# Loading the head of x through two engines, waiting last on GpSimd, and one semaphore for TensorE's events

## The chip, the cores and the metric

The kernel runs on one core of a Trainium2 chip. The metric is the device time of one execution in microseconds. Three runs of the kernel before took 180.77, 180.64 and 180.67 us, median 180.67. Its profiled execution took 180.69 us, of which the profile shows 178.9 us, from the first instruction to the last; its mean granted TensorE clock was 0.936.

## The reference

Eight experts, each a two-layer perceptron with a ReLU between, on 256 rows of its own:

```python
n_experts, capacity, hidden, expert_hidden = 8, 256, 512, 2048
h = np.matmul(x, w1)      # [8, 256, 512] x [8, 512, 2048]
h = np.maximum(h, 0)
return np.matmul(h, w2).astype(np.float32)   # x [8, 2048, 512]
```

Inputs and output are float32. The weights are 67 MB of HBM, x and the output 4.2 MB each.

## The kernel before

All of x and all weights are brought to bf16 on their way into SBUF. GpSimd's DMA queue casts while it copies; SyncE's and ScalarE's queues copy float32 as it is.

**Loading x.** Partition p holds 16 rows of x (R = 16). The first four of them, the *head* (HEAD = 4, 128 rows of 8 KB), go through SyncE's queue as float32 into x_head, and VectorE casts them into x_sb (L116 and L117). The other twelve, the *tail*, go through GpSimd's queue and are cast on the way (L131). x_sb is not a buffer of its own: it lies in slot 2 of the buffer of w2. Only after both stands the section whose order is written by hand (L118 on); all engines enter it when the cast is done.

**Loading the weights.** GpSimd issues twelve loads, in the order of the list `loads` (L169): w1 and w2 of experts 0 and 1 together, then of 2 and 3, then smaller ones; the last, half of w2 of expert 7, has the semaphore d_half. There are four slots for each of w1 and w2 (NS = 4). A load into a used slot waits for TensorE to be done with the slot's expert (L149 to L157), and the load of w2 for experts 2 and 3 waits for the transposes, which read x_sb. SyncE waits for each landing and passes it on to TensorE as a count (L123).

**TensorE.** First 64 transposes turn x_sb into xT through PSUM (L278 on); VectorE and ScalarE each copy half of the results out (L179). Then a loop over the experts: 64 matmuls of 128x256 make the hidden layer in four groups of PSUM (h_ps, two buffers), ScalarE applies the ReLU to each group (L213) into hT, and 32 matmuls of 128x512 make the output in o_ps, which VectorE copies to out_sb (L196); the last half of expert 7 is copied by ScalarE (L219). The code of an expert is a loop whose body is issued again from registers, so all matmuls stand at L252 in the profile.

**Semaphores.** TensorE's last matmul of a transposed half raises p_xt, of a hidden group p_h, of an output half p_o. They are counters that only rise in this program, and the others wait for constants. s_ident counts the two steps of making the identity matrix, v_out two moments at which VectorE's copies are drained.

**The end.** After expert 6, GpSimd stores the outputs of seven experts in one DMA (L172, 3.6 MB); a small store of 3 KB stands ahead of it (L160). SyncE stores expert 7's output when both of its halves are copied (L125). Then GpSimd drains (L423), ScalarE waits for all stores by d_pool and d_last (L424 and L425), and the closing barrier follows, in which SyncE gathers the other engines and GpSimd clears the semaphores.

The lines that matter for the change:

```python
nc.sync.dma_start(x_head[:], x_v[:, :HEAD * H])              # L116
nc.vector.tensor_copy(x_sb[:, :HEAD * H], x_head[:])         # L117
...
pool.drain()                                                 # L423
act.wait_ge(d_pool, 48)                                      # L424
act.wait_ge(d_last, 16).then_inc(s_ident)                    # L425
```

Of the kernel before, what the change touches and what calls it, by code (L numbers as in the profile page):

```python
# [8 lines left out]
FP32 = mybir.dt.float32  # L9
BF16 = mybir.dt.bfloat16  # L10
PE = mybir.EngineType.PE


FIRST_FREE = 16512 + 8192


@with_exitstack
def kernel(
# [7 lines left out]
    nc = tc.nc  # L26
    P = 128
    E, C, H = x.shape
    F = w1.shape[2]
    MC = C // P  # L30
# [27 lines left out]
    def allot(name, shape, dtype):  # L58
# [3 lines left out]
        free += math.prod(shape[1:]) * mybir.dt.size(dtype)  # L62
        return t

    w1_sb = allot("w1_sb", [P, NS, K1 * F], BF16)
    w2_sb = allot("w2_sb", [P, NS, K2 * H], BF16)
    xT = allot("xT", [P, K1, MC, E * P], BF16)
    hT = allot("hT", [P, K2, C], BF16)
    out_sb = allot("out_sb", [P, E, MC, H], FP32)
    identity = allot("identity", [P, P], BF16)  # L70
    W1_AT, W2_AT, XT_AT = places["w1_sb"], places["w2_sb"], places["xT"]

# [7 lines left out]
    def sem(name):  # L80
        return tc.alloc_semaphore(name)

    d_w1 = [sem(f"d_w1{i}") for i in range(NS)]
    d_w2 = [sem(f"d_w2{i}") for i in range(NS)]
    d_half, d_pool, d_last = sem("d_half"), sem("d_pool"), sem("d_last")

    s_ident = sem("s_ident")
    p_xt, p_h, p_o = sem("p_xt"), sem("p_h"), sem("p_o")  # L90
    v_out, v_last = sem("v_out"), sem("v_last")

    c_xt = [sem(f"c_xt{i}") for i in range(MC)]
    c_h, c_o, c_w1, c_w2 = sem("c_h"), sem("c_o"), sem("c_w1"), sem("c_w2")
# [10 lines left out]
    loads += [(1, (E - 1,), 0, 2), (2, (E - 1,), 0, 1), (2, (E - 1,), 1, 1)]  # L105
    landed, counts = [], {}
    for w, es, h, _ in loads:
        s = d_half if h else (d_w1, d_w2)[w - 1][es[0] % NS]
        counts[id(s)] = counts.get(id(s), 0) + 16
        landed.append((s, counts[id(s)]))  # L110

# [1 line left out]

    x_pool = ctx.enter_context(tc.tile_pool(name="x_pool", bufs=1))
    x_head = x_pool.tile([P, HEAD * H], FP32, tag="x_head")
    nc.sync.dma_start(x_head[:], x_v[:, :HEAD * H])  # L116
    nc.vector.tensor_copy(x_sb[:, :HEAD * H], x_head[:])  # L117
    with tc.tile_critical(no_gpsimd_drain=True):  # L118

        sp = nc.sync  # L120
        for i, (w, es, h, n) in enumerate(loads):
# [7 lines left out]

        pool = nc.gpsimd  # L130
        pool.dma_start(x_sb[:, HEAD * H:], x_v[:, HEAD * H:]).then_inc(d_pool, 16)  # L131
        pool.memset(identity[:], 0.0).then_inc(s_ident)  # L132
        pool.wait_ge(s_ident, 1)

        pool.affine_select(  # L135
            out=identity[:],
# [3 lines left out]
            base=0,  # L140
            pattern=[[-1, P]],
            channel_multiplier=1,
        ).then_inc(s_ident)
        for i, (w, es, h, n) in enumerate(loads):


            old = es[-1] - NS
            if w == 2 and 2 in es:
                tc.wait_critical_data_deps()  # L149
                pool.wait_ge(p_xt, K1 * MC)  # L150
            if old >= 0 and h == 0:
                if w == 1:
                    pool.wait_ge(p_h, NG * (old + 1))
                else:
                    pool.wait_ge(p_o, MC * (old + 1))
            if i == len(loads) - 1:


                pool.wait_ge(v_out, 1)
                pool.dma_start(  # L160
                    out_v[:16, 0:5:2, :16], out_sb[:16, 0:5:2, 0, :16]
                ).then_inc(d_pool, 16)
            e, ne, at_slot = es[0], len(es), es[0] % NS
            if w == 2:
                src = w2_v[:, e:e + ne, h:h + n, :].rearrange("p e h n -> p e (h n)")
                dst = w2_sb[:, at_slot:at_slot + ne, h * JH * H:(h + n) * JH * H]
            else:
                src, dst = w1_v[:, e:e + ne, :], w1_sb[:, at_slot:at_slot + ne, :]
            pool.dma_start(dst, src).then_inc(landed[i][0], 16)  # L169
        pool.wait_ge(v_out, 2)  # L170
        pool.wait_ge(d_pool, 32)
        pool.dma_start(  # L172
            out_v[:, :E - 1, :], out_sb[:, :E - 1].rearrange("p e m h -> p e (m h)")
# [12 lines left out]
        dve.sem_inc(c_xt[0], 1)  # L186
        dve.sem_inc(c_o, MC)
        for ko in range(K1):
            dve.wait_ge(p_xt, ko * MC + 1)
            copy_xt(dve.tensor_copy, ko, 0).then_inc(c_xt[0])  # L190
        for e in range(E):
            for m in range(MC):
                if e == E - 1 and m == 1:
                    break
                dve.wait_ge(p_o, e * MC + m + 1)
                cp = dve.tensor_copy(out_sb[:, e, m, :], o_ps[m][:])  # L196
                cp.then_inc(v_last if e == E - 1 else c_o)
            if e in (4, E - 2):
                dve.drain().then_inc(v_out)  # L199


        act = nc.scalar
        act.sem_inc(c_xt[1], 1)
        act.sem_inc(c_h, UG - 1)
        for ko in range(K1):
            act.wait_ge(p_xt, ko * MC + 2)
            copy_xt(act.copy, ko, 1).then_inc(c_xt[1])
        for e in range(E):
            if e:
                act.wait_ge(p_o, MC * e)  # L210
            for g in range(NG):
                act.wait_ge(p_h, e * NG + g + 1)
                act.activation(  # L213
                    hT[:, g * GJ:(g + 1) * GJ, :].rearrange("p a c -> p (a c)"),
                    h_ps[g % UG][:],
                    mybir.ActivationFunctionType.Relu,
                ).then_inc(c_h)
        act.wait_ge(p_o, E * MC)
        act.copy(out_sb[:, E - 1, 1, :], o_ps[1][:]).then_inc(v_last)  # L219


# [56 lines left out]
        def transposes():  # L278
            i = 0
            for m in range(MC):  # L280
                take(c_xt[m], 1)
                for r2 in range(R // MC):
                    if i % 6 == 0:
                        for k in range(i, min(i + 6, n)):
                            row = (k % (R // MC)) * MC + k // (R // MC)
                            pe.reg_add(bank[i // 6 % 2][k - i], reg["x"], row * H * 2)
                        if i + 6 > n:
                            pe.reg_add(reg["x"], reg["x"], 2)
                    t = matmul(
                        xt_ps[m][:, r2, :],  # L290
                        at(w2_sb, bank[i // 6 % 2][i % 6], [[K1, P]]),
                        pe.lower_ap(identity[:]),
                        start_tensor_calc=True,
                        stop_tensor_calc=True,
                        is_transpose=True,
                    )
                    i += 1
                t.then_inc(p_xt)

        pe.wait_ge(s_ident, 2)  # L300
        pe.wait_ge(d_pool, 16)
        x_first = X_AT + last_column(K1)
        pe.reg_mov(reg["x"], x_first)
# [48 lines left out]
        def half():  # L352
            n = JH * K1
            for i in range(n):
                j, ko = divmod(i, K1)
                c, r = place(CHUNKS1, i)
                if i == CHUNKS1[c][1] - 2:
                    if c + 1 < len(CHUNKS1):
                        next_chunk(CHUNKS1, c, address1)
                        if c + 2 == len(CHUNKS1):  # L360
                            pe.reg_add(reg["half"], reg["half"], 1)
                    else:
                        pe.reg_add(reg["b1"], reg["b1"], JH * 2)
                        first_addresses()
                        a, b, regs = CHUNKS2[0]
                        compute(address2, range(a, b), regs)
                g = j // GJ
                ends = j % GJ == GJ - 1 and ko == K1 - 1
                if ends:


                    take(c_h, 1)
                    if i == n - 1:
                        take(c_o, MC // 2)
                mm = matmul(
                    h_ps[g][:, (j % GJ) * C:(j % GJ + 1) * C],
                    at(w1_sb, r, [[K2, P]]),
                    at(xT, reg[f"xt{ko}"], [[E * P, MC], [1, P]]),
                    start_tensor_calc=ko == 0,
                    stop_tensor_calc=ko == K1 - 1,  # L380
                )
                if ends:
                    mm.then_inc(p_h)

        def expert():
            take(c_w1, 1)
            loop("half", reg["half"], 2, half)
            for k in range(K2):
                if k % JH == 0:
                    take(c_w2, 1)  # L390
                if k == K2 - GJ:

                    pe.wait_ge(c_h, UG - 1)
                c, r = place(CHUNKS2, k)
                if k == CHUNKS2[c][1] - 1 and c + 1 < len(CHUNKS2):
                    next_chunk(CHUNKS2, c, address2)
                if k == CHUNKS2[-1][0] - 1:
                    pe.reg_add(count, count, 1)
                    pe.reg_add(reg["half"], reg["half"], -2)
                if k == K2 - 1:  # L400
                    set_expert()
                for m in range(MC):
                    mm = matmul(
                        o_ps[m][:],
                        pe.lower_ap(hT[:, k, m * P:(m + 1) * P], for_matmul_weights=True),
                        at(w2_sb, r, [[1, H]]),
                        start_tensor_calc=k == 0,
                        stop_tensor_calc=k == K2 - 1,
                    )
                    if k == K2 - 1:  # L410
                        mm.then_inc(p_o)

        pe.reg_mov(count, 0)
        pe.reg_add(reg["half"], count, 0)
# [6 lines left out]


        pool.drain()  # L423
        act.wait_ge(d_pool, 48)  # L424
        act.wait_ge(d_last, 16).then_inc(s_ident)  # L425


# [28 lines left out]
```

## Time and profile before

| what | value |
|---|---|
| time, median of three runs | 180.67 us |
| span of the profile | 178.9 us |
| PE busy | 129.4 us (72%) |
| ScalarE busy | 38.7 us (22%) |
| VectorE busy | 15.8 us (9%) |
| moved by DMA, as written | 40.37 MB, of which GpSimd's queue 38.80 |
| HBM read | 71.30 MB |
| head of x, issue to landing | 4.9 us |
| tail of x, issue to landing | 11.6 us |
| last output (SyncE), issue to landing | 3.1 us |

A busy share is the time in which an engine worked, over the span. The time of a run is some 1.8 us longer than the span[...]. A load that is issued while others are queued shows a long time to its landing (48 us for the large weights): most of it is standing in the queue.

### The profile page before, as it was taken

The numbers are of one execution on the slowest core, as the hardware profiler recorded it, in microseconds if no ns is written. First come the engines' busy times: TensorE is split into PE (matmuls) and PEld (weight loads), VectorE is DVE, ScalarE is ACT, GpSimd is POOL, SyncE is SP. The second block draws the span as 40 slices with busy tenths as digits, with TensorE's granted clock in tenths as the row PEclk, the third lists the DMA queues.
The fourth block names the chain that finished last, engine by engine and source line by source line (L and its number), as shares of the span: only waits on it lengthen the run. The fifth ranks groups of instructions, "written<-read, shape, count | busy, mean of one in ns | idle before, by whom it ended". The sixth has DMA issues, their size and how long they took to land. (4 is left out here: it accounts for less than half of the span.)

```text
span 178.9 us, 2103 instructions
## 1 busy us (share of the span) xinstructions
PE 129.4 (72%) x832; PEld 90.5 (51%) x832; DVE 15.8 (9%) x20; ACT 38.7 (22%) x38; POOL 10.3 (6%) x21
## 2 busy tenths in 40 slices
PE   0008610793049999995079999999999999969990
PEld 0007610692013696594024884794695696359630
DVE  0204320000000200110000200200200200110010
ACT  0202420053000044044000251152062044004400
POOL 6100010000000002001000100100010000002000
PEclk9999999999756999999859999999999999987997
DMA  6999998999999999899899999999989999999995
GB/s 211 244 216 209 234 227 183 234 231 194 220 234 201 209 234 223 187 234 231 187 227 234 201 209 234 216 194 234 227 187 231 231 194 220 234 189 219 334 423 243
DMA packets 3744, 40.37 MB, mean 226 GB/s; under 512 B 288, under 2 KB 288, under 8 KB 1312
## 3 DMA queue, kind: packets, MB, share of 16 engines
q0 software_dynamic: 3456, 38.80, 97.2%
q1 hardware_dynamic: 288, 1.57, 2.4%
HBM read 71.30 MB, written 4.20 MB: 422 GB/s over the span
## 5 line engine op out<-in xcount | busy, mean ns | idle before, releaser
L252 PE MATMUL o_ps<-w_sb,hT 128*128 x256 | 61.3, 401 | 17.8 <-PEq L227 17.8
L252 PE MATMUL h_ps<-xT,w_sb 128*128 x512 | 62.2, 284 | 11.3 <-PEq L227 11.3
L252 PEld LDWEIGHTS h_ps<-xT,w_sb 128*128 x512 | 58.4, 146 | 15.9 <-issue 13.1
L213 ACT ACTIVATE hT<-h_ps 128x1024 bf16<-128x1024 f32 x32 | 32.7, 1023 | 111.2 <-PE h_ps L252 111.2
L252 PEld LDWEIGHTS o_ps<-w_sb,hT 128*128 128x128 bf16 x256 | 25.6, 102 | 50.7 <-issue 24.5
L196 DVE COPY out_sb<-o_ps 128x512 f32<-128x512 f32 x15 | 9.7, 686 | 141.2 <-PE o_ps L252 141.2
L252 PE MATMUL xt_ps<-identity,w_sb 128*128 128x128 bf16 x64 | 7.6, 311 | 15.6 <-PEq L227 15.6
L252 PEld LDWEIGHTS xt_ps<-identity,w_sb 128*128 x64 | 6.5, 146 | 16.4 <-issue 16.4
L169 POOL DMA_DIRECT2D w_sb<-in_w_dram x12 | 7.4, 619 | 105.1 <-PE h_ps L252 58.0
L179 ACT COPY xT<-xt_ps 128x1024 bf16<-128x1024 bf16 x4 | 4.0, 1012 | 11.7 <-PE xt_ps L252 11.7
L179 DVE COPY xT<-xt_ps 128x1024 bf16<-128x1024 bf16 x4 | 4.9, 1224 | 11.9 <-PE xt_ps L252 11.9
L172 POOL DMA_DIRECT2D out_dram<-out_sb x1 | 1.0, 966 | 33.3 <-DMA out_dram<-out_sb 33.3
L179 ACT ACT_TABLE_LOAD x1 | 1.3, 1283 | 7.2 <-DVE w_sb L117 7.2
L219 ACT COPY out_sb<-o_ps 128x512 f32<-128x512 f32 x1 | 0.6, 585 | 5.9 <-PE o_ps L252 5.9
L117 DVE CAST w_sb<-x_head 128x2048 bf16<-128x2048 f32 x1 | 1.2, 1227 | 5.6 <-DMA x_head<-in_x_dram 5.6
L160 POOL DMA_DIRECT2D out_dram<-out_sb x1 | 0.5, 549 | 14.8 <-DVEq L199 14.8
L131 POOL DMA_DIRECT2D w_sb<-in_x_dram x1 | 0.7, 679 | 0.8 <-POOLq L440 0.8
L135 POOL TENSOR_SCALAR_AFFINE_SELECT identity<-identity 128x128 bf16<-128x128 bf16 x1 | 0.3, 282 | 0.2 <-POOL identity L132 0.2
L132 POOL MEMSET identity<- 128x128 bf16 x1 | 0.2, 223 | 0.0
L440 POOL MEMSET const-float32-0.0<- 128x1 f32 x1 | 0.1, 93 | 0.2 <-issue 0.2
L440 POOL MEMSET const-bfloat16-1.0<- 128x1 bf16 x1 | 0.1, 95 | 0.0
L440 POOL MEMSET const-uint8-127<- 128x1 uint8 x1 | 0.1, 95 | 0.0
(1 smaller groups left out, 0.1 us busy)
## 6 DMA issues: line engine op xcount, KB each, us to landing
w_sb<-in_w_dram POOLq DMA_DIRECT2D x5, 4096.0 KB, 48.0
w_sb<-in_w_dram POOLq DMA_DIRECT2D x5, 2048.0 KB, 51.0
out_dram<-out_sb POOLq DMA_DIRECT2D x1, 3584.0 KB, 12.8
w_sb<-in_w_dram POOLq DMA_DIRECT2D x2, 1024.0 KB, 43.4
w_sb<-in_x_dram POOLq DMA_DIRECT2D x1, 1536.0 KB, 11.6
x_head<-in_x_dram SPq DMA_DIRECT2D x1, 1024.0 KB, 4.9
out_dram<-out_sb SPq DMA_DIRECT2D x1, 512.0 KB, 3.1
out_dram<-out_sb POOLq DMA_DIRECT2D x1, 3.0 KB, 33.8
```

What stands on the lines that cost most here:

```text
L117: nc.vector.tensor_copy(x_sb[:, :HEAD * H], x_head[:])
L131: pool.dma_start(x_sb[:, HEAD * H:], x_v[:, HEAD * H:]).then_inc(d_pool, 16)
L135: pool.affine_select(out=identity[:], in_=identity[:], compare_op=mybir.AluOpType.not_equal, fill=1.0, base=0, pattern=[[-1, P]], channel_ ...
L160: pool.dma_start(out_v[:16, 0:5:2, :16], out_sb[:16, 0:5:2, 0, :16]).then_inc(d_pool, 16)
L169: pool.dma_start(dst, src).then_inc(landed[i][0], 16)
L172: pool.dma_start(out_v[:, :E - 1, :], out_sb[:, :E - 1].rearrange("p e m h -> p e (m h)")).then_inc(d_pool, 16)
L179: return copy(xT[:, ko, m].rearrange("k (ep r2) -> k ep r2", r2=R // MC), xt_ps[m][:].rearrange("k r2 ep -> k ep r2"),)
L196: cp = dve.tensor_copy(out_sb[:, e, m, :], o_ps[m][:])
L213: act.activation(hT[:, g * GJ:(g + 1) * GJ, :].rearrange("p a c -> p (a c)"), h_ps[g % UG][:], mybir.ActivationFunctionType.Relu,).then_in ...
L219: act.copy(out_sb[:, E - 1, 1, :], o_ps[1][:]).then_inc(v_last)
L252: return pe.add_instruction(inst)
L440: nc = _bacc.Bacc("TRN2", target_bir_lowering=False, num_devices=1)
```

## The change

It has four parts.

1. The head of x is loaded in two halves of 64 partitions, one issued by SyncE and one by ScalarE. The purpose is to share out the issue of that transfer.
2. The wait for all stores at the end moves from ScalarE to GpSimd, which drains its queue there already.
3. One semaphore, s_pe, counts all of TensorE's events, in the order in which they happen: 8 transposed halves, then for each expert four hidden groups and two output halves. p_xt, p_h and p_o go, and with them ScalarE's extra wait on p_o ahead of each expert but the first, since a count of s_pe that includes the hidden group includes what came before it. s_event likewise takes the place of s_ident and v_out. An unused semaphore of w1's slot 1 goes too.
4. The buffers by hand begin 8 KB lower, and out_sb stands first among them, so that it shares its place with x_head, which is dead by the time of the first output.

```diff
-FIRST_FREE = 16512 + 8192
+FIRST_FREE = 16512
...
+    out_sb = allot("out_sb", [P, E, MC, H], FP32)
     w1_sb = allot("w1_sb", [P, NS, K1 * F], BF16)
...
-    out_sb = allot("out_sb", [P, E, MC, H], FP32)
...
-    s_ident = sem("s_ident")
-    p_xt, p_h, p_o = sem("p_xt"), sem("p_h"), sem("p_o")
-    v_out, v_last = sem("v_out"), sem("v_last")
+    s_event = sem("s_event")
+    s_pe, v_last = sem("s_pe"), sem("v_last")
+    def after_transposes(n):
+        return s_pe, n
+    def after_hidden(e, groups):
+        return s_pe, K1 * MC + e * (NG + MC) + groups
+    def after_outputs(e, halves):
+        return s_pe, K1 * MC + e * (NG + MC) + NG + halves
...
-    nc.sync.dma_start(x_head[:], x_v[:, :HEAD * H])
+    for engine, part in [(nc.sync, slice(0, P // 2)), (nc.scalar, slice(P // 2, P))]:
+        engine.dma_start(x_head[part], x_v[part, :HEAD * H])
     nc.vector.tensor_copy(x_sb[:, :HEAD * H], x_head[:])
...
                 if w == 1:
-                    pool.wait_ge(p_h, NG * (old + 1))
+                    pool.wait_ge(*after_hidden(old, NG))
                 else:
-                    pool.wait_ge(p_o, MC * (old + 1))
+                    pool.wait_ge(*after_outputs(old, MC))
...
         for e in range(E):
-            if e:
-                act.wait_ge(p_o, MC * e)
             for g in range(NG):
-                act.wait_ge(p_h, e * NG + g + 1)
+                act.wait_ge(*after_hidden(e, g + 1))
...
         pool.drain()
-        act.wait_ge(d_pool, 48)
-        act.wait_ge(d_last, 16).then_inc(s_ident)
+        pool.wait_ge(d_pool, 48).then_inc(s_event)
+        pool.wait_ge(d_last, 16).then_inc(s_event)
```

More of the change, by code (lines that the diff above doesn't have):

```diff
@@ L81, in sem @@
         return tc.alloc_semaphore(name)
-    d_w1 = [sem(f"d_w1{i}") for i in range(NS)]
-    d_w2 = [sem(f"d_w2{i}") for i in range(NS)]
-    d_half, d_pool, d_last = sem("d_half"), sem("d_pool"), sem("d_last")
-    s_ident = sem("s_ident")
-    p_xt, p_h, p_o = sem("p_xt"), sem("p_h"), sem("p_o")
-    v_out, v_last = sem("v_out"), sem("v_last")
+    d_w = {
+        (w, i): sem(f"d_w{w}_{i}")
+        for w, slots in [(1, (0, 2, 3)), (2, (0, 1, 2, 3))]
+        for i in slots
+    }
+    d_half, d_pool, d_last = sem("d_half"), sem("d_pool"), sem("d_last")
+    s_event = sem("s_event")
[6 more added lines that the diff above has]
+        return s_pe, K1 * MC + e * (NG + MC) + NG + halves
     c_xt = [sem(f"c_xt{i}") for i in range(MC)]
@@ L107 @@
     for w, es, h, _ in loads:
-        s = d_half if h else (d_w1, d_w2)[w - 1][es[0] % NS]
+        s = d_half if h else d_w[w, es[0] % NS]
         counts[id(s)] = counts.get(id(s), 0) + 16
@@ L131 @@
         pool.dma_start(x_sb[:, HEAD * H:], x_v[:, HEAD * H:]).then_inc(d_pool, 16)
-        pool.memset(identity[:], 0.0).then_inc(s_ident)
-        pool.wait_ge(s_ident, 1)
+        pool.memset(identity[:], 0.0).then_inc(s_event)
+        pool.wait_ge(s_event, 1)
         pool.affine_select(
@@ L142 @@
             channel_multiplier=1,
-        ).then_inc(s_ident)
+        ).then_inc(s_event)
         for i, (w, es, h, n) in enumerate(loads):
@@ L149 @@
                 tc.wait_critical_data_deps()
-                pool.wait_ge(p_xt, K1 * MC)
+                pool.wait_ge(*after_transposes(K1 * MC))
             if old >= 0 and h == 0:
                 if w == 1:
-                    pool.wait_ge(p_h, NG * (old + 1))
+                    pool.wait_ge(*after_hidden(old, NG))
                 else:
-                    pool.wait_ge(p_o, MC * (old + 1))
+                    pool.wait_ge(*after_outputs(old, MC))
             if i == len(loads) - 1:
-                pool.wait_ge(v_out, 1)
+                pool.wait_ge(s_event, 3)
                 pool.dma_start(
@@ L169 @@
             pool.dma_start(dst, src).then_inc(landed[i][0], 16)
-        pool.wait_ge(v_out, 2)
+        pool.wait_ge(s_event, 4)
         pool.wait_ge(d_pool, 32)
@@ L188 @@
         for ko in range(K1):
-            dve.wait_ge(p_xt, ko * MC + 1)
+            dve.wait_ge(*after_transposes(ko * MC + 1))
             copy_xt(dve.tensor_copy, ko, 0).then_inc(c_xt[0])
@@ L194 @@
                     break
-                dve.wait_ge(p_o, e * MC + m + 1)
+                dve.wait_ge(*after_outputs(e, m + 1))
                 cp = dve.tensor_copy(out_sb[:, e, m, :], o_ps[m][:])
@@ L198 @@
             if e in (4, E - 2):
-                dve.drain().then_inc(v_out)
+                dve.drain().then_inc(s_event)
         act = nc.scalar
@@ L205 @@
         for ko in range(K1):
-            act.wait_ge(p_xt, ko * MC + 2)
+            act.wait_ge(*after_transposes(ko * MC + 2))
             copy_xt(act.copy, ko, 1).then_inc(c_xt[1])
         for e in range(E):
-            if e:
-                act.wait_ge(p_o, MC * e)
             for g in range(NG):
-                act.wait_ge(p_h, e * NG + g + 1)
+                act.wait_ge(*after_hidden(e, g + 1))
                 act.activation(
@@ L217 @@
                 ).then_inc(c_h)
-        act.wait_ge(p_o, E * MC)
+        act.wait_ge(*after_outputs(E - 1, MC))
         act.copy(out_sb[:, E - 1, 1, :], o_ps[1][:]).then_inc(v_last)
@@ L297, in transposes @@
                     i += 1
-                t.then_inc(p_xt)
-        pe.wait_ge(s_ident, 2)
+                t.then_inc(s_pe)
+        pe.wait_ge(s_event, 2)
         pe.wait_ge(d_pool, 16)
@@ L382, in half @@
                 if ends:
-                    mm.then_inc(p_h)
+                    mm.then_inc(s_pe)
         def expert():
@@ L410, in expert @@
                     if k == K2 - 1:
-                        mm.then_inc(p_o)
+                        mm.then_inc(s_pe)
         pe.reg_mov(count, 0)
```

## The prediction

> **What bounds the kernel now.** I read the slices of the page first, then the DMA queues, then the timeline at both ends. From the page of before, the tenths of DMA busy time in 40 slices, and the two queues:
>
> ```profile
> DMA  6999998999999999899899999999989999999995
> ...
> q0 software_dynamic: 3456, 38.80, 97.2%
> q1 hardware_dynamic: 288, 1.57, 2.4%
> ```
>
> The 16 DMA engines are idle only in the first and the last slice. PE is busy 72% of the span and waits for weights, so the stream of packets is the bound. Its two ends show in stretches of 0.5 us (last columns: granted clock, DMA share, GB/s; a packet counts where it starts, so a share can pass 1):
>
> ```profile
> 1.00:1.50 0.50, 0.00 (x0) 0.00 (x0) 0.00 (x0) 0.00 (x0) 0.26 (x1) 1.00 0.00 0
> 1.50:2.00 0.50, 0.00 (x0) 0.00 (x0) 0.00 (x0) 0.00 (x0) 0.50 (x2) 1.00 1.04 164
> 2.00:2.50 0.50, 0.00 (x0) 0.00 (x0) 0.00 (x0) 0.00 (x0) 0.26 (x2) 1.00 0.47 115
> 2.50:3.00 0.50, 0.00 (x0) 0.00 (x0) 0.00 (x0) 0.00 (x0) 0.34 (x2) 1.00 0.84 311
> 3.00:3.50 0.50, 0.00 (x0) 0.00 (x0) 0.00 (x0) 0.00 (x0) 0.50 (x1) 1.00 1.08 459
> ...
> 176.50:177.00 0.50, 0.00 (x0) 0.00 (x0) 0.00 (x0) 0.00 (x0) 0.00 (x0) 0.62 0.96 393
> 177.00:177.50 0.50, 0.00 (x0) 0.00 (x0) 0.00 (x0) 0.00 (x0) 0.00 (x0) 0.50 0.15 57
> ```
>
> Nothing moves before 1.5 us, and full rate comes only at about 3 us; from there to 177.0 us there is no gap. So a microsecond at the start of the stream is a microsecond at its end. The packet records of the trace say it more sharply. [...] An 8 KB row of the head takes 0.309 us when warm. The first row of an engine begins between 1.739 and 2.492 us and takes 0.33 to 1.09 us, 0.716 on average. The engines finish their eight rows between 4.680 and 5.210 us, and on each the first packet of x's tail follows at once. At the other end the same engines finish the large output between 175.620 and 176.151 us: the spread of 0.53 us at the head is still there. What the slowest engine loses in the head is lost for good.
>
> The timeline shows who needs the head, and what follows the last matmuls:
>
> ```profile
> 0.74 0.38 SPq L116 DMA_DIRECT2D x_head<-in_x_dram  x1
> 1.24 0.68 POOL L131 DMA_DIRECT2D w_sb<-in_x_dram  x1 [0.79 <-POOLq L440]
> 5.62 1.23 DVE L117 CAST w_sb<-x_head 128x2048 bf16<-128x2048 f32 x1 [5.62 <-DMA x_head<-in_x_dram]
> 13.37 1.63 PEld L252 LDWEIGHTS xt_ps<-identity,w_sb 128*128 x16 [13.37 <-issue]
> ```
> ```profile
> 173.85 0.69 DVE L196 COPY out_sb<-o_ps 128x512 f32<-128x512 f32 x1 [16.60 <-PE o_ps L252]
> 174.06 0.58 ACT L219 COPY out_sb<-o_ps 128x512 f32<-128x512 f32 x1 [5.93 <-PE o_ps L252]
> 174.67 0.35 SPq L125 DMA_DIRECT2D out_dram<-out_sb  x1
> ```
>
> The cast is done at 6.85 us; PE starts at 13.37, when the tail of x has landed (12.9). So the head's own landing has over 6 us of slack; only the place it takes in the stream counts. The last output is issued at 174.67, and its first packets run at 175.63, right behind the first engine to finish the large output. The slowest engine takes them at 176.16, so PE has 0.53 us of slack at the end and the packets decide.
>
> [...] on each engine all rows of the head stand before all rows of the tail. [...] That is 0.38 us here (the SPq row), and it lies on the path, since the engines idle through it. [...] The trace shows 8 of 128 rows on each; I take 4 and 4. [...] No row of before has two issuers at once, so whether ScalarE must wait for SyncE isn't shown.
>
> **The change part by part.**
>
> 1. *Shorter issue.* One issue of 128 rows, 0.378 us, becomes two of 64, on SyncE and ScalarE, which both leave the start barrier at 0.66 us. If the time goes with the rows, each takes 0.19 us and the first packets start 0.19 us earlier; if it is fixed, nothing. (The 4 KB rows at L125, also 128, took 0.347: bytes don't set it.) I take 0.19; bounds 0 and 0.19.
>
> 2. *Earlier work for the later engines.* The first rows of 14 engines begin one after another over 0.405 us, about the length of the issue, so descriptors seem to be dealt out engine by engine. The engine that finishes last began 0.241 us after the first. With half as many rows to deal, half of that: 0.12 us. Bounds: 0, and the 0.33 us by which that engine lies behind the mean of 4.88 us.
>
> 3. *Extra completion packets.* One more for each engine, 0.009 us in the records, 0.006 by spacing: +0.006 us. The bytes are the same, so the stream is otherwise unchanged.
>
> 4. *The end.* ScalarE waited for the last output: landed 177.762, its wait 177.783, its drain 177.887, SyncE's NOP 177.970. On Pool, with 0.078 us between two of its semaphore instructions, the NOP comes at 177.86 and SyncE follows 0.083 later, at 177.94: −0.03 us. If both of Pool's waits are paid behind the landing, +0.05. Pool's drain at L423 ends at 177.20, before the landing, and hides. Behind Pool's new wait stand only the closing drain (0.047) and barrier, which wait for SyncE anyway.
>
> 5. *One counter for TensorE.* The same matmul still releases each waiter, so no wait moves. ScalarE drops seven extra waits on o_ps; it waits 111.2 us for PE on the h_ps rows, which hides them. s_event replaces s_ident and v_out at the same points. Three semaphores fewer in the closing clear, at 5 ns each in the records: −0.015.
>
> 6. *Addresses* of out_sb and the weights move. No row shows a cost by address; out_sb lies over x_head, dead since 6.85 us, while the first output copy is at 61 us or later (o_ps is first signalled at 61.3). The cast waits for two landings rather than one: 6 us of slack hide it.
>
> Sum: −0.19 − 0.12 + 0.006 − 0.03 − 0.015 = −0.35; 180.67 − 0.35 = 180.32 us.
>
> **The rivals.**
>
> *A, the forecast:* the stream starts earlier on every engine, 180.32. For it: the stream is dense from 3 to 177 us. Against: the 0.19 and the 0.12 rest on time in proportion to rows. With both at their upper bound (0.19 + 0.33) it would be 180.11, with half of both 180.47; the line of 0.2% is 180.31, in the midst of A.
>
> *B, the first reads are what is slow.* Engines that begin at 1.74 need 1.07 us for the first row, those that begin at 2.47 need 0.34; most first rows end near 2.5 to 2.9 us whenever they began. If that moment is set by the memory, an earlier start is swallowed: only the end's 0.04 remains, 180.63.
>
> *C, ScalarE's half is slow on its own account.* A second queue may pay a first row of its own, 0.716 − 0.309 = 0.41 us more on average and 0.78 at worst[...]. With 0.41 − 0.04 this gives 181.04, at the worst 181.41. Against it: four rows of SyncE's half last 1.2 us, longer than another issue of 0.38, and could hide the wait.
>
> A change of PE's clock I leave aside: a window at half clock covered 159.6 to 163.0 us of the last expert, and the three times still lie within 0.13 us.
>
> **How the numbers follow.** A has 0.65, of which I put 0.42 below the line and 0.23 above it, since the stream may gain more where several engines' slow first rows overlap; B 0.23; C 0.12. So faster 0.42, same 0.23 + 0.23 = 0.46, slower 0.12. The time is A's. The range goes from 179.95, somewhat below A's upper bound because first rows of up to 1.09 us could shrink too, to 180.95, which takes in B and the milder half of C.
>
> **What would show it.** Right: in the stretches of the changed kernel the rate at 1.5 to 3.0 us is higher, the slowest engine finishes the head about 0.3 us before 5.21, and the first weights and last weights land earlier by the same amount (PE's start moves from 13.37 to about 13.05). B: the first packets begin earlier and full rate still comes at 3 us. C: ScalarE's rows begin late, or a gap stands between the halves. Wrong altogether: the landings shift by one amount and the time by another, so that the end or PE decides.

## The result, and the profile after

The changed kernel took 182.88 us (median of four runs, 182.66 to 182.98), against 180.65 us for the kernel before: a ratio of 1.0120, 95% interval 1.0105 to 1.0136. It is 2.23 us slower, where 180.32 us was forecast.

The page of after, DMA busy in 40 slices and the queues (queue 1 is SyncE's, queue 10 ScalarE's):

```profile
DMA  5999999999999999999999999999999999999995
...
q0 software_dynamic: 3456, 38.80, 96.0%
q1 hardware_dynamic: 224, 1.05, 1.9%
q10 hardware_dynamic: 80, 0.52, 1.3%
```

The stream is as dense as before, and the two hardware queues carry the same 1.57 MB. But their packets now take 1.9 + 1.3 = 3.2% of the engines' time, where they took 2.4%. The timeline of after shows both issues, the tail's, the cast and PE's start:

```profile
0.74 0.55 ACTq L130 DMA_DIRECT2D x_head<-in_x_dram  x1
0.74 0.54 SPq L130 DMA_DIRECT2D x_head<-in_x_dram  x1
1.24 0.68 POOL L145 DMA_DIRECT2D w_sb<-in_x_dram  x1 [0.79 <-POOLq L452]
...
8.12 1.23 DVE L131 CAST w_sb<-x_head 128x2048 bf16<-128x2048 f32 x1 [8.12 <-DMA x_head<-in_x_dram]
15.69 1.63 PEld L264 LDWEIGHTS xt_ps<-identity,w_sb 128*128 x16 [15.69 <-issue]
```

An issue of 64 rows lasts 0.54 us, not the 0.19 that I had taken; the issue of 128 rows before lasted 0.38. The cast starts 2.50 us later and PE 2.32 us later. GpSimd does not wait for the cast, unlike what the section on the kernel before says of all engines: it issues the tail at 1.24 us in both kernels. So a late head delays the stream only by the place that its own packets take. The same stretches as in the prediction (last columns: DMA share and GB/s):

```profile
1.50:2.00 0.50, 0.00 (x0) 0.00 (x0) 0.00 (x0) 0.00 (x0) 0.50 (x2) 1.00 0.00 0
2.00:2.50 0.50, 0.00 (x0) 0.00 (x0) 0.00 (x0) 0.00 (x0) 0.26 (x2) 1.00 1.34 229
2.50:3.00 0.50, 0.00 (x0) 0.00 (x0) 0.00 (x0) 0.00 (x0) 0.35 (x2) 1.00 0.38 98
3.00:3.50 0.50, 0.00 (x0) 0.00 (x0) 0.00 (x0) 0.00 (x0) 0.50 (x1) 1.00 1.37 426
3.50:4.00 0.50, 0.00 (x0) 0.00 (x0) 0.00 (x0) 0.00 (x0) 0.50 (x2) 1.00 1.09 246
4.00:4.50 0.50, 0.00 (x0) 0.00 (x0) 0.00 (x0) 0.00 (x0) 0.50 (x2) 1.00 0.78 164
4.50:5.00 0.50, 0.00 (x0) 0.00 (x0) 0.00 (x0) 0.00 (x0) 0.50 (x1) 1.00 0.94 213
```

Nothing moves before 2 us. And where the kernel before had reached 459 GB/s, after rises to 426 at 3.0 us and falls to 164 to 246 GB/s, although the engines are busy all the while. The packet records give the size: first packets begin at 2.085 us (1.739 before). Once the stream runs, a row of 8 KB takes 0.61 us (median of ScalarE's 64), where it took 0.309 (median of all 128). ScalarE's rows come after SyncE's on each engine, by the order of the records: SyncE's half ends in 16 completion packets, the first three at 3.746, 3.972 and 4.268 us, and the first rows of ScalarE's follow at 3.752, 3.986 and 4.282. The head is done between 6.093 and 7.573 us, where it was 4.680 to 5.210.

The loss stays as it is until the end. The last weights land at 170.13 us (167.81 before), and the last lines of the timeline are those of before, 2.33 us later:

```profile
176.39 0.58 ACT L231 COPY out_sb<-o_ps 128x512 f32<-128x512 f32 x1 [5.93 <-PE o_ps L264]
177.00 0.35 SPq L139 DMA_DIRECT2D out_dram<-out_sb  x1
```

### The profile page after: what moved, and what is told of

Its sections match the earlier page's. It is cut to its first block, busy times and chain, and to the rows that moved or that the text cites. A ratio compares the mean times of both kernels' runs of the same rounds, so it can differ in the third digit from the quotient of the medians.

```text
span 181.2 us, 2097 instructions
## 1 busy us (share of the span) xinstructions
PE 127.2 (70%) x824; PEld 90.0 (50%) x832; DVE 15.8 (9%) x20; ACT 38.7 (21%) x38; POOL 10.3 (6%) x21
## 5 line engine op out<-in xcount | busy, mean ns | idle before, releaser
L264 PE MATMUL o_ps<-w_sb,hT 128*128 x248 | 59.6, 395 | 19.4 <-PEq L239 18.6
L264 PE MATMUL h_ps<-xT,w_sb 128*128 x512 | 61.5, 283 | 11.9 <-PEq L239 11.9
```

The costliest lines, as they stand in the source:

```text
L264: return pe.add_instruction(inst)
```

## The experiments

The theories, as the expectations name them. **P**: the rate goes with the partitions that a transfer writes. Rows into 0 to 63, and likewise into 64 to 127, take twice as long, rows into all 128 or into 32 to 95 do not. The factor of two is my estimate from the 0.61 us above against 0.309; for 32 to 95 it was a guess, with no run behind it yet. **Q**: two issuers or two queues disturb each other. **R**: another part of the change costs the time. **S**: a transfer of 64 rows is slow wherever it goes. **W** and **V** concern 0.2 us outside the span and come up on the way.

### The change without the split

```diff
-    for engine, part in [(nc.sync, slice(0, P // 2)), (nc.scalar, slice(P // 2, P))]:
-        engine.dma_start(x_head[part], x_v[part, :HEAD * H])
+    nc.sync.dma_start(x_head[:], x_v[:, :HEAD * H])
```

> The changed kernel with the head of x again loaded whole, by SyncE alone; the other three parts of the change stay (GpSimd waits last, one counter for TensorE, new addresses). Theory P ([...] each row takes twice as long): all of the loss lies in the split, so 180.6 us, 0 to 0.1 below the kernel before. Theory Q (two issuers disturb each other): the same 180.6. Theory R (the wait on GpSimd, the one counter or the addresses cost something): clearly above 180.8, up to 182.9 if they are the whole cause.

180.59 us, ratio 1.0001 (0.9986 to 1.0015). R falls: the wait on GpSimd, the counter and the addresses together change nothing that can be measured (the interval leaves 0.3 us either way). Its head begins and PE starts as in the kernel before (timeline):

```profile
0.74 0.38 SPq L129 DMA_DIRECT2D x_head<-in_x_dram  x1
...
13.33 1.63 PEld L263 LDWEIGHTS xt_ps<-identity,w_sb 128*128 x16 [13.33 <-issue]
```

### The split alone

The kernel before with the split of the head and nothing else:

```diff
-    nc.sync.dma_start(x_head[:], x_v[:, :HEAD * H])
+    for engine, part in [(nc.sync, slice(0, P // 2)), (nc.scalar, slice(P // 2, P))]:
+        engine.dma_start(x_head[part], x_v[part, :HEAD * H])
```

> The kernel before with the split of the head alone: partitions 0 to 63 by SyncE, 64 to 127 by ScalarE. Theories P and Q: 182.9, the whole loss; rows of the head at 0.6 us each after the first ones. Theory R: 180.6 to 181.

183.07 us, ratio 1.0138 (1.0120 to 1.0156): the whole loss. The head is done at 7.41 us on the slowest engine. So the cause is in the split; what of it, the next runs tell.

### Both halves by SyncE

```diff
-    for engine, part in [(nc.sync, slice(0, P // 2)), (nc.scalar, slice(P // 2, P))]:
+    for engine, part in [(nc.sync, slice(0, P // 2)), (nc.sync, slice(P // 2, P))]:
```

> The kernel before with the same two halves of 64 partitions, but both issued by SyncE, one after the other. Theory P: the rows still take 0.6 us each, and the time is 182.3 to 183.0, since the issuer does not matter. Theory Q (two issuers or two queues at once are the cause): no second issuer, rows at 0.31 us, 180.6 to 180.9.

182.29 us, ratio 1.0096 (1.0078 to 1.0115), at the lower edge of P's figures; Q as the sole cause, with one issuer and no loss, falls. The two issues last 0.545 and 0.580 us although nobody else issues, so the long issue belongs to the 64 rows and not to a second issuer. The first half's rows slow down as before: taken in the order of their starts, sixteen at a time, their medians are 0.78, 0.31, 0.51 and 0.63 us. The second half comes so late that the tail's packets stand among its own, and it lands at 12.3 us. There its rows took 0.42 to 0.46 us (medians by sixteen), not the 0.6 that P expected, and the loss is smaller than with two queues.

### Halves by columns

The kernel before; each half now writes all 128 partitions, in rows of 4 KB, on two queues:

```diff
-    nc.sync.dma_start(x_head[:], x_v[:, :HEAD * H])
+    for engine, part in [(nc.sync, slice(0, HEAD * H // 2)), (nc.scalar, slice(HEAD * H // 2, HEAD * H))]:
+        engine.dma_start(x_head[:, part], x_v[:, part])
```

> The kernel before with the head halved by columns: SyncE and ScalarE each load 1024 of the 2048 columns of all 128 partitions (rows of 4 KB, two queues). Theory P: all 128 partitions are written by each half, rows of 4 KB take 0.155 us, no loss but what a later start costs (up to 0.35 us): 180.5 to 181.0. Theory Q: two issuers, so 182 to 183.

181.24 us, ratio 1.0035 (1.0014 to 1.0056), a little above P's figures and far below Q's. Rows of 4 KB take 0.159 us at the median, about half of the 0.309 for 8 KB. The head is done at 5.10 us, 0.1 earlier than before, and yet the time is 0.6 longer, so I ran it again:

> The column split again, since its eight times were spread over 180.9 to 182.2. Its head was done at 5.10 us, 0.1 before that of the kernel before, and the loss of 0.6 us arose only between 90 and 120 us. If that was a disturbance from outside: 180.5 to 180.6 now. If the split itself causes it (two queues beside the weights' queue): again 181.2.

181.17 us, ratio 1.0027 (1.0020 to 1.0034). It is not a disturbance alone, then. This time the head is done at 5.35 us, and PE starts 0.08 us after that of the kernel before (timeline):

```profile
0.74 0.40 ACTq L117 DMA_DIRECT2D x_head<-in_x_dram  x1
0.74 0.38 SPq L117 DMA_DIRECT2D x_head<-in_x_dram  x1
...
13.45 1.63 PEld L253 LDWEIGHTS xt_ps<-identity,w_sb 128*128 x16 [13.45 <-issue]
```

Both issues last 0.38 to 0.40 us side by side: with 128 rows each, two issuers did not slow each other either (one alone took 0.38 in the kernel before), and neither waited for the other: both begin at 0.74 us. Each run gives its time and its span. The span's median is 179.1 us here and 178.9 in the kernel before; the time outside the span is 2.01 us here and 1.78 there. So about half of the 0.5 us is no work of the kernel's that the trace shows. The split alone had 2.00 outside, the changed kernel 1.78. What they differ in at the end is who waits last.

### Other 64 partitions

The kernel before, split so that SyncE's half is 32 to 95. By P, rows into these 64 keep their 0.31 us:

```diff
-    nc.sync.dma_start(x_head[:], x_v[:, :HEAD * H])
+    for engine, part in [(nc.sync, slice(32, 96)), (nc.scalar, slice(0, 32)), (nc.scalar, slice(96, 128))]:
+        engine.dma_start(x_head[part], x_v[part, :HEAD * H])
```

> The kernel before with the head split by partitions in another place: SyncE loads partitions 32 to 95, ScalarE loads 0 to 31 and 96 to 127 in two transfers. Theory P: [...] its rows of 8 KB take 0.31 us, while ScalarE's rows[...] take up to 0.6; the time lies between, 181.5 to 182.4. Theory S (any transfer of 64 or fewer rows is slow, wherever it goes): all rows at 0.6 us, 183 or more.

182.27 us, ratio 1.0089 (1.0070 to 1.0108). The time is where P had it, but this doesn't settle it: ScalarE's first transfer came ahead, the two mixed, and the median row of either queue took 0.48 us, neither 0.31 nor 0.6. Hence a cleaner form, by SyncE alone with 32 to 95 first:

```diff
+    for part in [slice(32, 96), slice(0, 32), slice(96, 128)]:
+        nc.sync.dma_start(x_head[part], x_v[part, :HEAD * H])
```

> The kernel before with the head in three transfers, all by SyncE: partitions 32 to 95 first, then 0 to 31, then 96 to 127. Its first transfer differs from the first one of the run with both halves by SyncE only in which 64 partitions it writes; there, the third and fourth rows of the engines took 0.51 and 0.63 us in the middle of 16. Theory P: [...] here the third and fourth rows take 0.31 us. Theory S (64 rows at a time are slow wherever they go): 0.5 to 0.63 again. The time says less, since the later transfers stand among the tail's packets: 181 to 182.3.

181.68 us, ratio 1.0052 (1.0040 to 1.0064). The first transfer's rows, sixteen at a time, took 0.67, 0.31, 0.31 and 0.32 us (medians). With 0 to 63 they took 0.78, 0.31, 0.51 and 0.63. Among the fourth sixteen no two overlap: each took 0.31 to 0.33 us here and 0.61 to 0.67 there. The stretches show where the rates part; first this kernel, then the one with both halves by SyncE:

```profile
3.00:3.50 0.50, 0.00 (x0) 0.00 (x0) 0.00 (x0) 0.00 (x0) 0.50 (x1) 1.00 0.84 328
3.50:4.00 0.50, 0.00 (x0) 0.00 (x0) 0.00 (x0) 0.00 (x0) 0.50 (x2) 1.00 1.14 385
```
```profile
3.00:3.50 0.50, 0.00 (x0) 0.00 (x0) 0.00 (x0) 0.00 (x0) 0.50 (x1) 1.00 1.36 426
3.50:4.00 0.50, 0.00 (x0) 0.00 (x0) 0.00 (x0) 0.00 (x0) 0.50 (x2) 1.00 0.81 172
```

From 3.5 us on, 32 to 95 stay fast and 0 to 63 fall off. The head's rows alone, without the tail's packets in the same stretch, are 311 against 148 GB/s. (One stretch earlier it is the other way round: the slow rate has not yet set in.) So S falls, and what P said of 32 to 95 came true. The long issue came back (0.61 us for these 64 rows), so it is another thing than the slow rows.

Two limits. The transfers to 0 to 31 and 96 to 127 in this kernel, each within one of the halves that are slow by P, ran among the tail's packets, with at most eleven rows under way at once, and their rows took only 0.32 us at the median. So writing to one half was not slow in itself here; the rows took about 0.6 us in the changed kernel, where all engines did it at once. Why 64 to 127 took 0.42 to 0.46 among the tail's packets above is open. And the partition and the place in HBM go together in every run here: partition p is always filled from the same 32 KB of x. No run loads other rows of x into 0 to 63. Whether the limit lies where the rows are written or where they are read is therefore not shown.

### A head of twice the size

The changed kernel, and the changed kernel with its head loaded whole, each with

```diff
-    HEAD = 4
+    HEAD = 8
```

> The changed kernel with a head of 8 rows per partition instead of 4 (twice the bytes through the two halves of 64 partitions, and fewer in the tail). Theory P: rows of 16 KB take 1.23 us rather than 0.62, so the loss against the whole head of the same size doubles, to about 4.5 to 5 us: 185.1 to 185.7. A fixed price for each transfer or queue: the loss stays at 2.3, 182.9.

> The same head of 8 rows per partition loaded whole by SyncE. All theories: rows of 16 KB take 0.62 us, the stream carries the same bytes, 180.4 to 180.8.

184.77 us (1.0220, 1.0203 to 1.0237) and 180.70 us (0.9999, 0.9990 to 1.0007). The loss by the split is 184.77 − 180.70 = 4.07 us for 2 MB, where it was 182.88 − 180.59 = 2.29 for 1 MB. My figure under P was 4.5 to 5, a bit too much, for two reasons. I doubled the later start too: it is paid once, and came again (first packets at 2.071 us). And ScalarE's rows, which now ran among the tail's packets, took 1.06 us on average, against 1.23 for SyncE's. Without the later start, 4.07 − 0.35 = 3.72 and 2.29 − 0.35 = 1.94, a factor of 1.92. So the rest grows with the bytes, which a fixed price for a transfer would not. Halved first, then whole, in stretches of 2 us:

```profile
4.00:6.00 2.00, 0.00 (x0) 0.00 (x0) 0.00 (x0) 0.00 (x0) 1.00 (x2) 1.00 1.00 205
```
```profile
4.00:6.00 2.00, 0.00 (x0) 0.00 (x0) 0.00 (x0) 0.00 (x0) 1.00 (x2) 1.00 0.96 340
```

The busy share is nearly the same, the rate is not (of the 340 GB/s, 61 are packets of the tail; the 205 are the head's alone). A busy share of the DMA engines says here how long packets took, not how much they moved.

### Who waits last

The 0.2 us outside the span. **W**: it arises where ScalarE has issued a transfer and also waits last for the stores. **V**: where ScalarE has issued one, whoever waits. Three kernels: the changed one with columns in place of rows, and the kernel before with the whole head issued by ScalarE, without and with the wait on GpSimd. The diff is that of the last one.

```diff
-    nc.sync.dma_start(x_head[:], x_v[:, :HEAD * H])
+    nc.scalar.dma_start(x_head[:], x_v[:, :HEAD * H])
...
-        act.wait_ge(d_pool, 48)
-        act.wait_ge(d_last, 16).then_inc(s_ident)
+        pool.wait_ge(d_pool, 48).then_inc(s_ident)
+        pool.wait_ge(d_last, 16).then_inc(s_ident)
```

> The changed kernel with its head halved by columns (all 128 partitions in each half, SyncE and ScalarE), so that GpSimd waits last. The column split in the kernel before took 181.17 us, 0.5 more, though its span grew by 0.2 only; the rest of 0.23 us lay outside the span. Theory W (that rest arises where ScalarE has issued a transfer and also waits last): it goes, 180.8 to 180.95. Theory V (ScalarE's transfer costs it whoever waits): again 181.1 to 181.2.

> The kernel before with the whole head issued by ScalarE instead of SyncE, nothing else. Rows of 8 KB at 0.31 us as before and the same span, 178.9. Theory W and theory V: 0.2 us more outside the span, 180.9. If the rest comes from two hardware queues rather than from ScalarE's: 180.67, except that SyncE's last store is a second queue too.

> The same as the run with the head by ScalarE, and with the wait for all stores on GpSimd as in the changed kernel. Theory W: 180.67, nothing outside the span beyond the 1.78 us of the kernel before. Theory V: 180.9.

| kernel | ScalarE issues | waits last | us | ratio (interval) | outside the span |
|---|---|---|---|---|---|
| before | no | ScalarE | 180.65 | 1 | 1.78 |
| columns, rest of before | half | ScalarE | 181.17 | 1.0027 (1.0020 to 1.0034) | 2.01 |
| columns, rest of the change | half | GpSimd | 180.74 | 1.0003 (0.9995 to 1.0011) | 1.75 |
| rows, both halves by SyncE | no | ScalarE | 182.29 | 1.0096 (1.0078 to 1.0115) | 1.88 |
| 32 to 95 first, all by SyncE | no | ScalarE | 181.68 | 1.0052 (1.0040 to 1.0064) | 1.85 |
| whole by ScalarE | all | ScalarE | 180.82 | 1.0013 (1.0006 to 1.0019) | 1.86 |
| whole by ScalarE | all | GpSimd | 180.66 | 1.0000 (0.9992 to 1.0008) | 1.77 |

Half of W holds: with the wait on GpSimd the rest goes, most plainly in the last two rows, which differ in nothing else, and V falls. Its size is 0.08 us in one case and 0.23 in the other, and the case with 0.08 was expected at 0.2; the columns with GpSimd waiting came out at 180.74, a little under W's 180.8 to 180.95. The other half of W does not hold. In the two kernels with all of the head by SyncE, ScalarE issued no transfer, and yet about 0.1 us came on top of the 1.75 to 1.76 of the kernel before that ran beside them. So with ScalarE waiting last, each other way of loading the head that was tried cost something outside the span, whoever issued it. What happens in that time the trace doesn't show, so its mechanism stays open. No version came out faster than the kernel before; with columns and the rest of the change the two are alike.

## Why the prediction was wrong, point by point

**The bound was read rightly.** The stream of packets decides, and what it loses at the start arrives at the end: the slowest engine was 2.36 us later with the head, PE started 2.32 later, the last weights landed 2.32 later, the span grew by 2.3. The spread between engines also stays: 1.48 us at the head, and 1.48 at the end of the large output (177.01 to 178.49).

**Step 3 failed: "The bytes are the same, so the stream is otherwise unchanged."** I priced the extra completion packet at 0.006 us and took the rows at 0.309. The rows took 0.551 us on average in SyncE's half and 0.595 in ScalarE's, against 0.369 for the whole head: 4 × 0.551 + 4 × 0.595 − 8 × 0.369 = 1.63 us for each engine. (Four rows of a half for each engine is a mean, 64 over 16; queue 10's 80 packets are ScalarE's 64 rows and 16 completion packets.) I had looked at which engines a half uses, and not at which partitions it writes. The runs with 32 to 95 against 0 to 63 (third and fourth rows 0.31 and 0.32 us against 0.51 and 0.63), and with columns against rows (0.159 us for 4 KB against 0.61 for 8 KB), show that it depends on which partitions a transfer covers; why, the runs leave open.

**Step 1 had the wrong sign.** An issue was to shrink with its rows, from 0.38 to 0.19 us. It grew to 0.54, which is 0.16 longer, and the first packets came 0.35 later, not 0.19 earlier; my bounds of 0 and 0.19 left that side out. The rest of the 0.35 is not explained. With 1.63 + 0.35 = 1.98 us one has about the loss of the mean engine, 1.94 us (from 4.91 to 6.85 us; I had written 4.88 for the mean before). The other 0.4 us is the slowest engine's share in a wider spread.

**Step 2** expected the engines to come closer together. They came apart, from 0.53 to 1.48 us.

**Step 4** priced the end at −0.03 us. In the trace the last landing and the gathering barrier lie 0.355 us apart before (177.762 to 178.117) and 0.358 after (180.085 to 180.443): GpSimd's side is quicker (SyncE's NOP comes 0.159 us after the landing, where it came 0.208 after it), but SyncE now waits for the two halves' semaphores in two steps (180.289 and 180.351; before in one, 178.021). I had not seen what this part is good for: beside a head that is loaded in another way, it takes away the rest outside the span.

**Steps 5 and 6** held as far as can be seen: nothing beyond 0.3 us, by the run without the split.

**The rivals.** C ended on the right side, with another cause. It had a second cold first row, or a wait of ScalarE for SyncE. ScalarE's rows were slow from the first to the last (0.60, 0.54, 0.61 and 0.63 us by sixteens), and both issues ran side by side (0.55 and 0.54 us, from 0.74 on). B had the rate at 3 us right, 426 GB/s, but its first packets were to come earlier, not later, and it had no fall after it: luck. The order that the trace of before shows for head and tail holds for the halves too: they stand one after the other on each engine, and the rows of each also run at about half the rate (0.62 us in the last sixteen of SyncE's and 0.63 of ScalarE's, against 0.309).

## What to carry to other kernels

Before splitting a transfer in two, ask which partitions each part writes, not only how many engines carry it: here a row of 8 KB into 64 to 127 took 0.61 us, and 0.309 where the transfer covered all 128. The busy share of the DMA engines does not show it (1.00 at 205 GB/s, 0.96 at 340). Splitting by columns kept the rate (4 KB in 0.159 us). Here the DMA engines were busy for 90% or more of every slice but the first and the last, and the 2.36 us that the slowest engine lost in the first transfer came back as 2.3 us of span, although the cast of that data was done at 9.35 us and PE started only at 15.69.

## What was not expected of the hardware

- An issue of 64 rows lasted 0.54 to 0.61 us and one of 32 rows 0.39 to 0.56, against 0.35 to 0.40 for 128 rows, of 8 KB or of 4 KB, whether or not another engine issued at the time. No run here says why.
- The slow rate sets in with a delay: with both halves by SyncE, second rows into 0 to 63 still took 0.31 us, the third 0.51, the fourth 0.63. No run here says why.
- Where the head was loaded in another way than in the kernel before and ScalarE waited last, the time outside the span was about 0.1 to 0.3 us longer; where GpSimd waited last, it was 1.75 to 1.81 us throughout.
